# Measured durations in the planner of a two-layer hybrid decoder trunk

## The chip, the cores and the metric

The kernel runs on one core of a Trainium2 chip. The time is the device time of one execution in microseconds (us), and a version is judged by the median of its runs.

## What is computed

A decoder trunk of two layers on 512 tokens of width 1024, all in float32. The reference, cut to what matters:

```python
def hybrid_mixer(h, ...):
    proj = h @ w_in                       # 1024 -> q, k, v, z, xbc, dt
    q = partial_rotary(q); k = partial_rotary(k)
    attn = dilated_attention(q, k, v)     # 8 query heads on 2 kv heads
    xbc = jax.nn.silu(causal_depthwise_conv(xbc, conv_w, conv_b))
    dt = jax.nn.softplus(dt + dt_bias)
    y = ssd_chunked(xs, dt, -jnp.exp(a_log), bm, cm) + d_skip * xs
    y = rmsnorm(y * jax.nn.silu(z), ssm_norm)   # in two groups of 512
    return jnp.concatenate([attn, y], axis=-1) @ w_out

def reference(x, ...):
    h = x
    for layer in range(2):
        h = h + hybrid_mixer(rmsnorm(h, norm_mix), ...)
        t = rmsnorm(h, norm_ffn)
        h = h + (jax.nn.silu(t @ w_gate) * (t @ w_up)) @ w_down   # hidden width 2816
    return rmsnorm(h, final_norm)
```

## The kernel before

Features lie on the partitions and the 512 tokens along the free axis. A weight piece of 128 columns and an operand are each split into a rounded part and a rest (`whi` and `wlo`, `xh` and `xl`), and a k-tile of a product takes three matmuls of 128x128 by 128x512: `xh,whi`, `xl,whi`, `xh,wlo`. ScalarE makes `whi`, VectorE makes `wlo`. `block` (line 506) writes one output tile `acc` in units of two k-tiles, six matmuls. Nearly all of TensorE's work is such units.

In a layer the input projection comes first, in pieces, and in between stand the small products of the state space part (`ssd`: tiles `ee`, `xdt`, `hold`), of the gate (`gate`) and of attention (`scores`, `values`). The gate multiplies `xbc` by `z` on GpSimd, squares the products on ScalarE (`sq`), adds the squares on GpSimd, sums them over the partitions by a small matmul (`tr<-ones,sq`), makes `var` on VectorE and `rcol` (a power) on GpSimd, and spreads `rcol` to a row by four transposes (`tr<-ident,rcol`). In attention each head's scores (`tr<-kh,qs2` and `tr<-kl,qs2`) go through a reduction on VectorE (`sa`, `mx`), an exponential with a sum on ScalarE (`sa`, `den`), a reciprocal and a scaling on VectorE. Four scaled heads are transposed (`tr<-ident,sa`), copied to SBUF by ScalarE (`pt`), multiplied with the values (`hold<-pt,vk`), and split into `ath` (ScalarE) and `atl` (VectorE). During attention, units of the output projection fill TensorE: parts r = 1 and 2 (eight output tiles each, of two units) need no attention result, part r = 0 needs `ath` and `atl` of all four token blocks.

The order of all this is not written by hand. Every operation is put in a list with an engine, an assumed duration, a priority number and the tiles that it reads and writes. `schedule` (line 217) plays the list on a simple model of the engines: whenever an engine is free in the model, it takes the ready operation of the lowest number, if the pools have room. The order of starts in the model is the order in which the instructions are emitted, and on the chip each engine runs its own list in that order, waiting at each instruction for what it needs. The priority of a projection unit is `clock[0]`, which goes on by an assumed duration per matmul; the other operations have numbers that are set relative to it (`at`). So an assumed duration never takes time on the chip: it only moves instructions in the engines' lists. The pools bound how far one engine can run ahead: three `acc` and three `tr` banks in PSUM, three `whi` and three `wlo` tiles.

The durations stand in `dcost` (line 375; VectorE and GpSimd), `act` (line 408; ScalarE), `block` and `finish` (matmuls of 512 columns) and at the two powers on GpSimd (lines 554 and 1150).

Of the kernel before, what the change touches and what calls it, by code (L numbers as in the profile page):

```python
# [33 lines left out]
KTOK = 4  # L34
# [15 lines left out]
# columns of the constant array  # L50
# [3 lines left out]
# columns of the transposed parameter rows  # L54
# [32 lines left out]
# The program is written as a list of operations on virtual tiles. A list schedule over a simple  # L87
# model of the engines fixes the order in which they are emitted; every engine then runs its
# instructions in that order.
# [69 lines left out]
class VTile:  # L159
    """A tile that gets its place when its first operation is emitted."""  # L160
# [22 lines left out]
class Plan:  # L183
# [33 lines left out]
    def schedule(self, reserve, near):  # L217
        """Start times by a list schedule: per engine the ready operation of the lowest priority
        number, with the slots of the pools and the loads of activation tables in the model."""
# [3 lines left out]
        engines = {}  # L223
# [5 lines left out]
        first = {}  # L229
# [37 lines left out]
        order = []  # L267
# [55 lines left out]
def hybrid_trunk(  # L323
# [50 lines left out]
    # ---- operations  # L374
    def dcost(eng, o, ins, fast=False, ptrs=0):
        n = o.free
        if eng == "pool":
            return 2.25e-3 * n + 0.07
        psum = any(isinstance(v, View) and v.tile.psum for v in [o] + ins)
        return (0.52e-3 if fast and not psum else 1.04e-3) * n + 0.065 + 0.06 * (ptrs > 0)  # L380
# [27 lines left out]
    def act(o, a, func, scale=None, bias=None, accum=None):  # L408
# [15 lines left out]
        cost = 0.83e-3 * o.free + (0.053 if a.tile.psum else 0.093) + 0.093 * len(ptr)  # L424
        plan.add("act", cost, outs, [a] + ptr, fn, table=TABLE.get(func))

    def mms(outs, prods, each, prio=None):
        """prods: (out, lhsT, rhs, start, stop), or (out, in, identity) for a transpose."""
# [40 lines left out]
    # A chunk is one load; its pieces, 128 columns each, are split into float32r parts hi + lo.  # L469
# [36 lines left out]
    def block(segs, lead=LEAD, t=None, total=None, done=0):  # L506
        """One output tile: segs of (weight piece, operands, first and last k-tile)."""
        t = acc() if t is None else t
        total = total or sum(k1 - k0 for _, _, k0, k1 in segs)
        for pid, xl, k0, k1 in segs:  # L510
# [5 lines left out]
            for ka in range(k0, k1, 2):  # L516
# [8 lines left out]
                mms([t], pr, 0.2165, clock[0])  # L525
                clock[0] += len(pr) * 0.2165
# [4 lines left out]
    hT = [C([P, S], f"hT{k}") for k in range(KD)]  # L531

    class Norm:
        """Sum of squares over feature tiles, then 1/rms per token, as a row on all partitions."""
# [12 lines left out]
        def col(self):  # L547
# [6 lines left out]
            plan.add("pool", 0.96, [self.r], [v, nhalf],  # L554
# [19 lines left out]
    # the first operands, out of the token-major input  # L574
# [56 lines left out]
    # coefficient -exp(a_log) on the rows of the heads, zero on the others  # L631
# [10 lines left out]
    # d_skip spread over the 64 features of a head: column l * 8 + j for feature tile j  # L642
# [16 lines left out]
    # selectors in float32r: row of a head to its 64 features, and the fixed halves of the  # L659
    # operands of the decay products  # L660
# [77 lines left out]
    def layer(l, xs, norm):  # L738
# [13 lines left out]
        # x, B, C through the convolution  # L752
# [15 lines left out]
        if l == 0:  # L768
            # the second half of the input arrives while its first half is in use
# [6 lines left out]
        # dt: the 16 columns sit on the first 16 rows of each quadrant, their low parts on the others  # L776
        M = {}

        def dt_chain():
# [35 lines left out]
            # token-major dt and dt * exp(last - cumulative)  # L815
# [11 lines left out]
            # decay over a whole chunk, on all partitions  # L827
# [26 lines left out]
        # ---- state space part of a group of heads  # L854
# [60 lines left out]
        def gate(g, ta):  # L915
            """Gate and grouped norm; leaves y / rms in place of x."""
# [26 lines left out]
        # ---- attention operands  # L943
# [248 lines left out]
```

## Time and profile before

| what | us |
|---|---|
| runs before: median of 3 (lowest, highest) | 1343.31 (1338.26, 1344.51) |
| span of the profiled execution, first to last instruction | 1336.7 |
| mean granted TensorE clock, as a share of full speed | 0.995 |
| TensorE busy | 1310.3 |
| VectorE busy | 789.0 |
| ScalarE busy | 608.4 |
| GpSimd busy | 143.2 |

For the profiled execution the page gives the span and no longer time. The lowest run lies 1.6 us above that span, the median 6.6 us. A busy TensorE isn't one at its peak, since the ends of matmuls are modelled: a projection matmul is shown with 0.39 us, while the next one starts 0.23 us later. Layer 0's mixer (projection, state space part, attention) runs to about 300 us in the trace, its SwiGLU to about 680, layer 1's mixer to about 955, its SwiGLU and the final norm to the end. Names in the trace leave out the numbers of the tiles.

### The profile page before, as it was taken

The page shows a single profiled execution, that of the slowest core. Times are in us where ns is not written, and L with a number is a line of the kernel's source. Part 1 is how long each engine was busy: PE and PEld are TensorE (multiplying, and loading weights), DVE is VectorE, ACT ScalarE, POOL GpSimd, SP SyncE. Part 2 cuts the span into 40 slices and gives each one's busy share as a digit, 9 for nine tenths or more (in the row PEclk, how much of TensorE's full clock was granted, in tenths as well). Part 3 has the DMA queues.
Part 4 walks back from the last instruction along what each step waited for, and adds up shares of the span by engine and source line. Part 5 has one row for each costly group of instructions (what it writes and reads, how often), then busy time and mean ns, then how long its engine had stood idle before and what let it go on. Part 6 is the DMA issues. An engine that isn't in the chain of part 4 may idle for free.

```text
span 1336.7 us, 15604 instructions
## 1 busy us (share of the span) xinstructions
PE 1310.3 (98%) x6118; PEld 1053.4 (79%) x6118; DVE 789.0 (59%) x1312; ACT 608.4 (46%) x956; POOL 143.2 (11%) x111
## 2 busy tenths in 40 slices
PE   7999998999999999999999999999999999999997
PEld 6778777678888888888888777767788888888876
DVE  5996689766444334444469687887744433344443
ACT  5878755654332223223347686466532222232233
POOL 1002456000000000000000235520000000000000
PEclk9999999999999999999999999999999999999999
DMA  5221111222222232222322221111332323332141
GB/s 176 95 95 64 63 63 32 64 63 95 95 95 75 96 129 95 95 87 96 117 84 76 67 92 64 38 58 38 91 115 84 97 74 102 111 123 67 61 160 63
DMA packets 111744, 115.46 MB, mean 86 GB/s; under 512 B 4492, under 2 KB 102072, under 8 KB 111672
## 3 DMA queue, kind: packets, MB, share of 16 engines
q1 hardware_dynamic: 111672, 114.47, 26.7%
q8 instruction: 48, 0.79, 0.3%
q14 instruction: 24, 0.20, 0.0%
HBM read 112.37 MB, written 2.10 MB: 86 GB/s over the span
## 4 chain that ended last, share of the span: by engine, by line
PE 89%; DVE 5%; ACT 2%; POOL 2%; issue 1%; DMA 1%; SPq 0%; POOLq 0%; DVEq 0%; ACTq 0%
PE acc L436 79%; PE tr L436 4%; PE tr L434 3%; PE hold L436 3%; DVE qs L384 1%; DVE xbc L395 1%; DVE wlo L384 1%; ACT whi L421 1%; POOL qr L384 0%; DMA raw<-in_w_down_dram 0%; POOL xbc L384 0%; DMA x<-in_x_dram 0%; DVE qs L949 0%; DVE sa L390 0%; DVE sa L1007 0%
## 5 line engine op out<-in xcount | busy, mean ns | idle before, releaser
L436 PE MATMUL acc<-xh,whi 128*128 128x512 f32 x1584 | 628.2, 397 | 1.4 <-ACT whi L421 1.1
L436 PE MATMUL acc<-xl,whi 128*128 128x512 f32 x1584 | 618.6, 391 | 0.0
L436 PE MATMUL acc<-xh,wlo 128*128 128x512 f32 x1568 | 613.2, 391 | 0.3 <-DVE wlo L384 0.3
L421 ACT CAST whi<-raw 128x1024 fp32r<-128x1024 f32 (+4 forms) x260 | 224.0, 867 | 490.3 <-PE acc L436 455.9
L436 PEld LDWEIGHTS acc<-xh,whi 128*128 128x128 f32 x1584 | 298.3, 188 | 66.8 <-issue 5.5
L436 PEld LDWEIGHTS acc<-xh,wlo 128*128 128x128 f32 x1568 | 295.0, 188 | 64.2 <-DVE wlo L384 1.5
L436 PEld LDWEIGHTS acc<-xl,whi 128*128 128x128 f32 x1584 | 298.5, 188 | 59.2 <-issue 0.5
L384 DVE TENSOR_TENSOR wlo<-raw,whi 128x1024 fp32r<-128x1024 f32 (+4 forms) x251 | 258.7, 1035 | 63.0 <-ACT whi L421 62.3
L384 DVE TENSOR_TENSOR ga<-acc,rstd 128x512 f32<-128x512 f32 x44 | 30.4, 692 | 182.4 <-PE acc L436 181.8
L384 DVE TENSOR_TENSOR hT<-hT,acc 128x512 f32<-128x512 f32 x80 | 54.8, 685 | 109.0 <-PE acc L436 108.3
L423 ACT ACT_TABLE_LOAD x54 | 69.3, 1283 | 6.4 <-DVE pmix L401 3.5
L555 POOL TENSOR_TENSOR rcol<-var,nhalf 128x4 f32<-128x4 f32 x8 | 8.7, 1091 | 558.3 <-DVE var L390 558.3
L395 DVE SCALAR_TENSOR_TENSOR xbc<-cu,cvp,xbc 128x511 f32<-128x511 f32 (+2 forms) x72 | 58.5, 816 | 3.2 <-ACT xbc L423 2.3
L384 DVE TENSOR_TENSOR up<-acc,rstd 128x512 f32<-128x512 f32 x44 | 30.3, 688 | 45.0 <-PE acc L436 44.9
L421 ACT CAST xh<-ga 128x512 fp32r<-128x512 f32 x44 | 27.4, 623 | 58.4 <-DVE ga L384 58.4
L423 ACT ACTIVATE sa<-sa,mx 128x512 f32<-128x512 f32 (+3 forms) x64 | 36.0, 562 | 36.6 <-DVE mx L1007 35.1
L1151 POOL TENSOR_TENSOR fr<-fvar,nhalf 128x1 f32<-128x1 f32 x4 | 2.2, 547 | 356.9 <-DVE fvar L390 356.9
L384 DVE TENSOR_TENSOR xl<-ga,xh 128x512 fp32r<-128x512 f32 x44 | 30.3, 688 | 15.1 <-ACT xh L421 15.1
L1007 DVE CUSTOM_DVE_ANT_0 sa<-tr,cst 128x512 f32<-128x512 f32 (+3 forms) x64 | 30.5, 477 | 10.3 <-PE tr L436 10.1
L384 DVE TENSOR_TENSOR ga<-ga,up 128x512 f32<-128x512 f32 x44 | 30.3, 689 | 3.7 <-ACT ga L423 1.4
L384 DVE TENSOR_TENSOR ee<-ee,cbm 128x512 f32<-128x512 f32 x32 | 26.0, 817 | 6.9 <-ACT ee L423 6.9
L384 POOL TENSOR_TENSOR xbc<-xbc,er 128x384 f32<-128x384 f32 x16 | 20.1, 1258 | 83.3 <-DVE er L384 43.1
(203 smaller groups left out, 1184.9 us busy)
## 6 DMA issues: line engine op xcount, KB each, us to landing
raw<-in_w_in_dram SPq DMA_DIRECT2D x25, 1024.0 KB, 5.0
raw<-in_w_gate_dram SPq DMA_DIRECT2D x20, 1024.0 KB, 5.2
raw<-in_w_up_dram SPq DMA_DIRECT2D x20, 1024.0 KB, 5.3
raw<-in_w_down_dram SPq DMA_DIRECT2D x16, 768.0 KB, 4.3
raw<-in_w_out_dram SPq DMA_DIRECT2D x8, 1024.0 KB, 4.9
raw<-in_w_down_dram SPq DMA_DIRECT2D x12, 640.0 KB, 4.4
raw<-in_w_out_dram SPq DMA_DIRECT2D x8, 512.0 KB, 5.0
x<-in_x_dram SPq DMA_DIRECT2D x8, 256.0 KB, 4.6
```

Source lines behind the costliest of these rows:

```text
L384: lambda: ENG[eng].tensor_tensor(R(o), R(a), R(b), alu))
L395: lambda: nc.vector.scalar_tensor_tensor(R(o), R(a), R(s), R(b), op0, op1))
L421: nc.scalar.copy(R(o), R(a))
L423: nc.scalar.activation(R(o), R(a), func, **kw)
L434: nc.tensor.transpose(R(p[0]), R(p[1]), R(p[2]))
L436: nc.tensor.matmul(R(p[0]), R(p[1]), R(p[2]), start=p[3], stop=p[4])
L555: lambda: nc.gpsimd.tensor_tensor(R(self.r), R(v), R(nhalf), ALU.pow))
L1007: nc.vector.tensor_tensor_reduce(R(sa[:, 0:nk]), R(t[:, 0:nk]), R(cst[:, C_MASK + S - nk:C_MASK + S]), 1.0, 3e38, ALU.add, ALU.min, R(m))
L1151: lambda r=r, v=v: nc.gpsimd.tensor_tensor(R(r), R(v), R(nhalf[:, 0:1]), ALU.pow))
```

## The change

Only the durations that the plan assumes are other numbers. A matmul of 512 columns goes from 0.2165 to 0.2267 us, both as a duration and as the step of `clock[0]`. A VectorE operation gets a fixed part of 0.155 us in place of 0.065, and its fast form (one input, SBUF to SBUF) isn't assumed any more where a per-partition scalar is read. A ScalarE operation gets 0.10 us more. The two powers on GpSimd go from 0.96 to 1.09 and from 0.30 to 0.55 us. GpSimd's other operations, the scores' matmuls and the reductions keep theirs. The list of operations is the same. The diff (lines in which only a comment was taken out are not shown):

```diff
     def dcost(eng, o, ins, fast=False, ptrs=0):
...
-        return (0.52e-3 if fast and not psum else 1.04e-3) * n + 0.065 + 0.06 * (ptrs > 0)
+        return (0.52e-3 if fast and not psum and not ptrs else 1.042e-3) * n + 0.155 + 0.04 * (ptrs > 0)
...
-        cost = 0.83e-3 * o.free + (0.053 if a.tile.psum else 0.093) + 0.093 * len(ptr)
+        cost = 0.84e-3 * o.free + (0.155 if a.tile.psum else 0.19) + 0.1 * len(ptr)
...
-                mms([t], pr, 0.2165, clock[0])
-                clock[0] += len(pr) * 0.2165
+                mms([t], pr, 0.2267, clock[0])
+                clock[0] += len(pr) * 0.2267
...
-            plan.add("pool", 0.96, [self.r], [v, nhalf],
+            plan.add("pool", 1.09, [self.r], [v, nhalf],
...
-            plan.add("pool", 0.3, [r], [v, nhalf],
+            plan.add("pool", 0.55, [r], [v, nhalf],
```

What it does to the order is seen in the engines' lists. The list of weight loads keeps its order. In both SwiGLU parts and in the final product TensorE's list is the same, up to the first units after attention; all that moves lies in the two mixers, and the second layer moves much as the first. Three places follow, all in layer 0. In the names of these lists the first number tells tiles of one kind apart and is the same in both kernels; a second number counts tiles in the order of emission.

The first is ScalarE at the first gate's squares (`sq_291`, `sq_292`; `whi_237` is a coming weight piece, `xbc_223` a convolution that waits for VectorE). Before:

```order
L421 CAST whi_233_1266<-raw_203_1120 128x1024
L423 ACTIVATE xbc_223_1279<-cu_222_1269,cvp_61_361 128x512
L423 ACTIVATE sq_291_1284<-xbc_178_743 128x512
L423 ACTIVATE ee_352_1286<-tr_351_1271 128x512
L423 ACT_TABLE_LOAD
L423 ACTIVATE ee_352_1286<-ee_352_1286 128x512
L423 ACT_TABLE_LOAD
L423 ACTIVATE xbc_223_1279<-xbc_223_1279,cvp_61_361 128x512
L421 CAST whi_237_1325<-raw_203_1120 128x1024
L423 ACTIVATE sq_292_1327<-xbc_183_849 128x512
```

And the same engine and place in the changed kernel:

```order
L421 CAST whi_233_1272<-raw_203_1105 128x1024
L423 ACTIVATE xbc_223_1277<-cu_222_1274,cvp_61_359 128x512
L423 ACTIVATE ee_352_1290<-tr_351_1281 128x512
L423 ACT_TABLE_LOAD
L423 ACTIVATE ee_352_1290<-ee_352_1290 128x512
L423 ACTIVATE sq_291_1307<-xbc_178_773 128x512
L423 ACTIVATE sq_292_1316<-xbc_183_821 128x512
L421 CAST whi_237_1320<-raw_203_1105 128x1024
L423 ACTIVATE ee_359_1330<-tr_358_1305 128x512
```

The last square now stands before the convolution `xbc_223` and before the weight cast, where it stood behind both.

The second place is TensorE at the sum of the second gate's squares (`tr_397`), where attention's scores begin (`tr_420`, `tr_422`). Before:

```order
L436 MATMUL tr_397_1956<-ones_7_74,sq_393_1587 128x1 x4
L436 MATMUL tr_420_1969<-kh_306_1657,qs2_335_1915 128x512
L436 MATMUL tr_420_1969<-kl_307_1678,qs2_335_1915 128x512
L436 MATMUL acc_542_1940<-xh_530_1443,whi_543_1895 128x512
L436 MATMUL acc_542_1940<-xl_531_1457,whi_543_1895 128x512
L436 MATMUL acc_542_1940<-xh_530_1443,wlo_544_1898 128x512
L436 MATMUL acc_542_1940<-xh_532_1484,whi_543_1895 128x512
L436 MATMUL acc_542_1940<-xl_533_1491,whi_543_1895 128x512
L436 MATMUL acc_542_1940<-xh_532_1484,wlo_544_1898 128x512
L436 MATMUL tr_422_1986<-kh_306_1657,qs2_336_1919 128x512
L436 MATMUL tr_422_1986<-kl_307_1678,qs2_336_1919 128x512
L434 MATMUL tr_400_1994<-ident_1_72,rcol_399_1982 128x128 x4
```

And now, from the same sum on:

```order
L436 MATMUL tr_397_1952<-ones_7_74,sq_393_1593 128x1 x4
L436 MATMUL acc_542_1939<-xh_530_1440,whi_543_1895 128x512
L436 MATMUL acc_542_1939<-xl_531_1456,whi_543_1895 128x512
L436 MATMUL acc_542_1939<-xh_530_1440,wlo_544_1906 128x512
L436 MATMUL acc_542_1939<-xh_532_1458,whi_543_1895 128x512
L436 MATMUL acc_542_1939<-xl_533_1488,whi_543_1895 128x512
L436 MATMUL acc_542_1939<-xh_532_1458,wlo_544_1906 128x512
L436 MATMUL tr_420_1976<-kh_306_1645,qs2_335_1915 128x512
L436 MATMUL tr_420_1976<-kl_307_1666,qs2_335_1915 128x512
L436 MATMUL acc_545_1983<-xh_526_1416,whi_546_1903 128x512
```

The unit of `acc_542` stands ahead of the scores `tr_420`; behind the row of `acc_545` come five more of that unit, then `tr_400`, and `tr_422` follows it. So twelve projection matmuls lie between the sum and `tr_400`, where six did. From here on, units of the output projection are taken earlier throughout attention: by the first `hold<-pt,vk` eleven of them, where it was seven.

The third place is TensorE at the end of attention: the scores of the last head (`tr_519`), the last transposes (`tr_524`), the last product with the values (`hold_521`), and the first unit that needs all of attention (`acc_596`). Before, behind `tr_519`:

```order
L436 MATMUL tr_519_2617<-kh_306_1657,qs2_343_1966 128x128
L436 MATMUL tr_519_2617<-kl_307_1678,qs2_343_1966 128x128
L436 MATMUL acc_585_2599<-xh_564_2060,whi_586_2471 128x512
L436 MATMUL acc_585_2599<-xl_565_2081,whi_586_2471 128x512
L436 MATMUL acc_585_2599<-xh_564_2060,wlo_587_2488 128x512
L436 MATMUL acc_585_2599<-xh_566_2076,whi_586_2471 128x512
L436 MATMUL acc_585_2599<-xl_567_2133,whi_586_2471 128x512
L436 MATMUL acc_585_2599<-xh_566_2076,wlo_587_2488 128x512
L436 MATMUL acc_588_2633<-xh_560_2026,whi_589_2516 128x512
```

Six matmuls of `acc_588` then stand before `tr_524`, six between it and `hold_521`, and six of `acc_591` between `hold_521` and `acc_596`. In the changed kernel there are none of these:

```order
L436 MATMUL acc_591_2592<-xh_566_2086,wlo_593_2513 128x512
L436 MATMUL tr_519_2654<-kh_306_1645,qs2_343_1964 128x128
L436 MATMUL tr_519_2654<-kl_307_1666,qs2_343_1964 128x128
L434 MATMUL tr_524_2675<-ident_1_72,sa_514_2619 128x128
L434 MATMUL tr_524_2675<-ident_1_72,sa_516_2636 128x128
L434 MATMUL tr_524_2675<-ident_1_72,sa_518_2664 128x128
L434 MATMUL tr_524_2675<-ident_1_72,sa_520_2669 128x128
L436 MATMUL hold_521_2682<-pt_523_2650,vk_313_1670 64x512
L436 MATMUL hold_521_2682<-pt_525_2680,vk_313_1670 64x512
L436 MATMUL acc_596_2692<-ath_402_2277,whi_597_2526 128x512
```

`acc_591`, the last tile that needs no attention, ends just before `tr_519`, and nothing stands between the last links of the chain. On VectorE the list behind `acc_591` reads, in the changed kernel:

```order
L384 TENSOR_TENSOR hT7_18_234<-hT7_18_234,acc_591_2592 128x512
L384 TENSOR_TENSOR wlo_610_2661<-raw_594_2274,whi_609_2657 128x512
L1011 RECIPROCAL den_503_2548<-den_503_2548 128x1
L1007 ISA sa_518_2664,mx_504_2542<-tr_517_2626,cst_60_322 128x128
L1007 ISA mx_504_2542 128x1
L390 TENSOR_SCALAR sa_516_2636<-sa_516_2636,den_503_2548 128x128
L1011 RECIPROCAL den_503_2548<-den_503_2548 128x1
L1007 ISA sa_520_2669,mx_504_2542<-tr_519_2654,cst_60_322 128x128
L1007 ISA mx_504_2542 128x1
L390 TENSOR_SCALAR sa_518_2664<-sa_518_2664,den_503_2548 128x128
L1011 RECIPROCAL den_503_2548<-den_503_2548 128x1
L390 TENSOR_SCALAR sa_520_2669<-sa_520_2669,den_503_2548 128x128
```

These are the steps that make the four scaled heads which `tr_524` transposes, and an addition into the residual (`hT7`) and a weight split (`wlo_610`) stand at their head. Before, the same steps stood behind `hT4` and `wlo_593`, two output tiles earlier.

## Rows read from the trace of the kernel before

**Rows 1.** The page: span, and busy time of each engine.
```profile
span 1336.7 us, 15604 instructions
PE 1310.3 (98%) x6118; PEld 1053.4 (79%) x6118; DVE 789.0 (59%) x1312; ACT 608.4 (46%) x956; POOL 143.2 (11%) x111
```

**Rows 2.** Chain of waits over the whole span: start, duration, what.
```profile
322.44 354.99 PE acc L436 x1566
```

**Rows 3.** What TensorE waited for: total us, times, longest.
```profile
PE tr L436 <- POOL sq L384: 3.8, 4, 1.0
PE tr L436 <- ACT rstd L421: 1.4, 2, 0.7
```

**Rows 4.** Stretches: length, busy per engine (count), granted clock, DMA share, GB/s.
```profile
145.00:149.00 4.00, 4.00 (x21) 2.95 (x20) 2.64 (x5) 3.12 (x5) 2.08 (x2) 0.57 0.40 139
...
220.00:224.00 4.00, 3.18 (x9) 1.92 (x8) 3.90 (x11) 2.53 (x5) 1.32 (x1) 0.57 0.00 0
224.00:236.00 12.00, 11.32 (x57) 9.34 (x58) 11.91 (x27) 9.24 (x19) 5.71 (x4) 1.00 0.00 1
...
270.00:290.00 20.00, 20.00 (x100) 14.40 (x100) 12.13 (x50) 10.11 (x32) 0.00 (x0) 1.00 0.23 53
...
800.00:804.00 4.00, 4.00 (x28) 2.65 (x24) 2.46 (x4) 2.42 (x4) 2.53 (x3) 1.00 0.18 62
```

**Rows 5.** Timeline at the first gate, layer 0: start, duration, instruction, [idle before].
```profile
132.10 1.30 POOL L384 TENSOR_TENSOR xbc<-xbc,z 128x512 f32<-128x512 f32 x1
...
137.02 1.74 POOL L384 TENSOR_TENSOR xbc<-xbc,z 128x512 f32<-128x512 f32 x1
141.61 1.77 POOL L384 TENSOR_TENSOR sq<-sq,sq 128x512 f32<-128x512 f32 x1 [2.85 <-ACT sq L423]
...
139.34 0.72 ACT L423 ACTIVATE xbc<-xbc,cvp 128x512 f32<-128x512 f32 x1 [1.54 <-DVE xbc L395]
...
140.90 0.63 ACT L423 ACTIVATE sq<-xbc 128x512 f32<-128x512 f32 x1
...
142.04 0.40 PE L436 MATMUL acc<-xh,wlo 128*128 128x512 f32 x1
143.44 1.05 PE L436 MATMUL tr<-ones,sq 128*128 128x1 f32 x8 [1.00 <-POOL sq L384]
```

**Rows 6.** Timeline at the second gate, layer 0.
```profile
216.92 1.05 PE L436 MATMUL tr<-ones,sq 128*128 128x1 f32 x8 [0.93 <-POOL sq L384]
...
219.29 0.47 PE L436 MATMUL tr<-kh,qs 128*128 128x512 f32 x1 [1.32 <-DVE mx L1007]
...
222.37 0.15 DVE L390 TENSOR_SCALAR var<-tr 128x4 f32<-128x4 f32 x1
...
222.60 1.32 POOL L555 TENSOR_TENSOR rcol<-var,nhalf 128x4 f32<-128x4 f32 x1 [2.94 <-DVE var L390]
...
223.97 0.65 PE L434 MATMUL tr<-ident,rcol 128*128 128x128 f32 x4 [0.82 <-POOL rcol L555]
```

**Rows 7.** Timeline at the end of attention, layer 0.
```profile
279.32 0.68 DVE L384 TENSOR_TENSOR hT<-hT,acc 128x512 f32<-128x512 f32 x1
...
282.56 0.29 DVE L390 TENSOR_SCALAR sa<-sa,den 128x128 f32<-128x128 f32 x1
...
283.78 0.60 PE L434 MATMUL tr<-ident,sa 128*128 128x128 f32 x4
...
284.41 0.59 ACT L421 COPY pt<-tr 128x512 f32<-128x512 f32 x1 [1.37 <-PE tr L434]
...
285.71 1.08 PE L436 MATMUL hold<-pt,vk 128*64 128x512 f32 x4
...
286.86 0.43 ACT L421 CAST ath<-hold 128x128 fp32r<-128x128 f32 x2 [0.61 <-PE hold L436]
...
288.12 0.69 DVE L384 TENSOR_TENSOR atl<-hold,ath 128x128 fp32r<-128x128 f32 x3 [0.50 <-ACT ath L421]
...
291.00 0.62 ACT L421 CAST whi<-raw 128x512 fp32r<-128x512 f32 x1 [2.91 <-PE acc L436]
```

More of the change, by code (lines that the diff above doesn't have):

```diff
@@ L1138, in finish @@
                 for u in range(0, len(pr), 6):
-                    mms([t], pr[u:u + 6], 0.2165, clock[0])
-                    clock[0] += 6 * 0.2165
+                    mms([t], pr[u:u + 6], 0.2267, clock[0])
+                    clock[0] += 6 * 0.2267
                 at(clock[0])
```

## The prediction

> **What bounds the kernel now.** I read the page first: TensorE is busy in 1310.3 of 1336.7 us [rows 1], so only what stops TensorE can move the end. The chain of waits says the same: one piece of it is 1566 projection matmuls in 354.99 us [rows 2], 0.2267 us each with nothing between. Such stretches hold both SwiGLU parts, and there the order does not change. What can be won or lost lies in the two mixers, in TensorE's stops. The list of what TensorE waited for names the first: the sum of the gate's squares, four times, 3.8 us [rows 3], one at each gate of each layer. The stretches show what comes with a stop: behind the one at 142 us, and behind those at 216 to 219 us, the granted clock is 0.57 over 4 us [rows 4]. That is 3.4 us at the half level (1.2 GHz), and it costs up to 1.7 us where matmuls would run densely; I count 1.5. In layer 1 the first gate's stop has no such fall behind it (granted 1.00 at 800 to 804 us, [rows 4]). The timelines then give the details of three places, in which the order changes most.
>
> **Removed: the stop at the first gate.** TensorE's last projection matmul before it starts at 142.04, the next could start 0.23 later, and the sum starts at 143.44 [rows 5]: a stop of 1.2 us. It waited for GpSimd's last addition (141.61 to 143.38), this for ScalarE's square at 140.90, and this stood behind a convolution step at 139.34 and a weight cast, though its input, GpSimd's product, was done at 137.02 + 1.74 = 138.76 [rows 5]. In the new list the square stands ahead of both. GpSimd's six operations can then follow each other without the 2.85 us pause, and end 2.85 earlier, at 140.5. They start about one unit (6 x 0.2267 = 1.36 us) later, because the hold that feeds them stands one unit later in TensorE's list: 141.9. TensorE reaches the sum one unit later too, less the transposes that were moved behind it, at about 141.7. So some 0.2 us of the stop is left, a gain of 1.0, and in layer 0 the clock stays up, 1.5 more. Bounds: nothing gained (the stop is as long as before) and 1.2 + 1.7. I take 2.5 us in layer 0 and, with no fall to save, 1.0 in layer 1.
>
> **Moved: the second gate.** The sum starts at 216.92 in both orders: GpSimd, VectorE and ScalarE have the same order there, and TensorE waits for them. Behind it, `rcol` ends at 222.60 + 1.32 = 223.92, since `var` is at 222.37 behind the same VectorE instructions [rows 6]. TensorE had two pairs of scores and one unit to do until then; now it has one pair and two units. That is 1.36 more and 0.5 less, 0.9 gained. The stop of 0.7 behind `rcol`, for the row `rstd` [rows 3], is filled by the other pair and the next unit, 0.7 more: 1.6 us per layer. Bounds: 0 and 3.2 (the stops of 1.32, 0.82, 0.7 and some of the clock).
>
> **Moved: filler that VectorE must feed.** By the first product with the values the new order has used four more units. Each needs its `wlo` from VectorE (0.68 to 0.69 us, as in [rows 7] for a 512-wide operation with two inputs), and VectorE is busy 11.91 of 12 us there [rows 4]. So 4 x 0.68 = 2.7 us of its work now stands ahead of the scores' reductions, and TensorE's `tr` banks come free later. Some of it is met by slack, because the same reductions were early before; bounds 0 and 2.7, and I take 0.75 per layer, nearer to nothing since TensorE did not wait for these reductions after 226 us.
>
> **Added: the end of attention.** Before, TensorE is busy 20 of 20 us here [rows 4], because 24 projection matmuls stand between the last links. Now there are none, and the chain shows. VectorE starts with the addition of `hT7`, just when the last unit ends; then come `wlo_610`, two reductions, three reciprocals and three scalings. ScalarE must first cast `whi_609`, which waits for the last unit, since it takes the tile that this unit reads: the same cast is seen waiting for TensorE at 291.00 [rows 7]. The same VectorE sequence, with `hT4` and `wlo_593` at its head, ran in 279.32 to 282.85, 3.53 us [rows 7]. TensorE has 0.17 us of scores to do beside it. That leaves a stop of 3.5 us (0.15 of latencies on both sides). Then the transposes: their copy starts 0.63 after them and takes 0.59, so the second half of `hold` starts 1.22 after the transposes and not 0.9: 0.3. Then `ath` begins 1.15 behind the start of `hold`, and the second `atl` is done about 1.55 behind that (288.12 + 0.29 - 286.86) [rows 7], and it is needed by the fifth matmul of the first unit, which would have been issued 1.0 + 4 x 0.23 = 1.9 behind the start of `hold`, not 2.7: 0.9. Together 4.7 us per layer, hidden before by the filler and by nothing now. Bounds: 1.3 + 1.2 = 2.5, if only the last head's reduction, exponential and scaling (1.3 of the 3.5) come late; and 6. A stop three times as long as the one at 142 should also bring the clock down: 1.5 more per layer, bounds 0 and 3.
>
> **The sum.** Layer 0: -2.5 - 1.6 + 0.75 + 4.7 + 1.5 = +2.85. Layer 1: -1.0 - 1.6 + 0.75 + 4.7 + 1.5 = +4.35. Together +7.2 us, a span of 1343.9 for 1336.7. The runs lie 1.6 to 7.8 above that span; the median 6.6 above. Against the median of 1343.3 this is 1350.5, slower by 0.5%. The three fewer loads of activation tables (1.28 us each, on ScalarE) and the moves in the first 130 us are set at nothing: VectorE has room behind dense TensorE work there, and without that cover they would be worth about a us either way. The last product's and the final norm's lists do not move.
>
> **Rivals.**
> First, not slower: the reductions of the last heads are done early. If TensorE's stops up to there let VectorE get ahead, only the last head is late at the end of attention: 2.5 in place of 4.7, and with a short stop no fall of the clock: 3.7 less per layer, -0.2 in all, 1343. For it: VectorE has 8 us of slack in 20 there [rows 4]. Against it: the additions `hT7` and `wlo_610` stand ahead of the reductions in its list, and cannot start before the last unit ends. It decides where the stop before the last transposes is under 1.5 us.
> Second, faster: besides this, the second gate gives its full 3.2 and VectorE's lag is nothing: -0.2 - 2 x 1.6 - 2 x 0.75 = -4.9, and with 1.0 more at the gates of the state space part -7: 1336.
> Third, slower still: the stop at the first gate stays. GpSimd's product of one shape took 1.30 us at 132.10 and 1.74 at 137.02 [rows 5], beside a VectorE that was busier; the change leaves GpSimd's assumed durations and this spread as they are. If the now unbroken run of six meets VectorE's convolutions and ends 1.2 later than I count, the gain of 3.5 is gone: +10.7, 1354. The Trainium skill ("SBUF — State Buffer", section "Who interferes with whom") has a rule by which this would come about: a VectorE operation with two inputs in SBUF and a GpSimd operation that reads SBUF block each other for the whole instruction, so one duration for each can't be right. The two durations of one shape agree with that rule.
> Fourth, slower still: VectorE's lag costs its 2.7 and the clock stays low longer behind the last stop (3 in place of 1.5): +7.2 + 2 x 1.95 + 2 x 1.5 = +14, 1357.
>
> **How the numbers follow.** Forecast, +3 to +11 around 1350.5: 0.50. First rival 0.20, second 0.12, third 0.10, fourth 0.08. About 0.5% (6.7 us) is what a measurement of this kernel can tell from no change. Of the forecast's 0.50, 0.30 lies above that and 0.20 below it; the third and fourth are slower; the first is the same but for 0.05 faster; of the second 0.08 is faster. That makes slower 0.48, the same 0.39, faster 0.13. Range 1338 to 1358; the forecast's own 1346 to 1354.
>
> **What would show it.** In the changed profile: a TensorE wait of 3 us or more for the scaling (`sa`, line 390) before the last transposes, in each layer, near 285 and 940 us, and a granted clock near 0.6 behind it; no wait for the gate's `sq` at 142 and granted 1.00 behind it; the wait for `mx` at 219 gone, that for `rcol` still there. The forecast is wrong if the stop at the end of attention is under 1.5 us, or if TensorE stops elsewhere for more than 5 us in all that it did not before.

## The result and the profile after

The changed kernel takes 1348.22 us (median of 9 runs, 1347.07 to 1350.85), the kernel before 1341.52 us (9 runs, 1337.33 to 1344.69). The ratio is 1.0058, with a 95% interval of 1.0040 to 1.0075: slower by 0.6%, where 1350.5 was forecast. The runs of the kernel before lie in two groups, near 1338 and near 1343.5, and its profiled execution is one of the lower; spans are therefore compared below with spans, and medians by the ratio to runs of the kernel before on the same chip.

The page of the changed kernel:

```profile
span 1345.3 us, 15613 instructions
PE 1310.8 (97%) x6118; PEld 1052.2 (78%) x6118; DVE 797.6 (59%) x1312; ACT 602.9 (45%) x953; POOL 145.7 (11%) x111
```

Against [rows 1], TensorE is busy as long as before (1310.8 us for 1310.3), and the span is 8.6 us longer: nearly all of it is time in which TensorE stood still. What it waited for, over the whole span (total us, times, longest; a cut):

```profile
PE hold L436 <- DVE ee L384: 6.3, 7, 2.3
PE tr L434 <- DVE sa L390: 4.8, 6, 1.3
PE tr L434 <- POOL rcol L555: 4.0, 3, 1.6
...
PE tr L436 <- POOL sq L384: 1.8, 2, 0.9
```

Two of the four waits for the gate's squares of [rows 3] are gone (3.8 us then, 1.8 now), and the waits for `rstd` and `mx` too. New are the waits for `sa`, three in each layer, and the longer ones for `ee` and `rcol`.

To see where each microsecond goes, I add up what TensorE loses: the time from the start of one matmul to the next, less the usual step of that kind of matmul (the lower quartile of its steps in these two traces). In dense stretches it is nearly nothing; around short matmuls some is left in every kernel, so only differences count. A matmul slowed by a lower clock counts as a loss too. In us, both layers added where nothing else is said:

| stretch | before | after | difference | forecast |
|---|---|---|---|---|
| start to first gate, layer 0 | 18.45 | 20.99 | +2.5 | 0 |
| first gates (layer 0, layer 1) | 4.27 + 2.89 | 1.63 + 2.49 | -2.6, -0.4 | -2.5, -1.0 |
| state space part between the gates | 13.89 | 17.66 | +3.8 | 0 |
| second gates | 14.72 | 11.38 | -3.3 | -3.2 |
| attention, to the last scores | 23.82 | 23.60 | -0.2 | +1.5 |
| end of attention (layer 0, layer 1) | 1.36 + 1.37 | 6.86 + 5.97 | +5.5, +4.6 | +6.2, +6.2 |
| the rest | 10.71 | 9.58 | -1.1 | 0 |
| sum | 91.5 | 100.2 | +8.7 | +7.2 |

The forecast for the ends of attention holds its 1.5 us of clock. The end of attention in the changed kernel, layer 0 (start, duration, instruction, [idle before]):

```profile
287.92 0.28 DVE L390 TENSOR_SCALAR sa<-sa,den 128x128 f32<-128x128 f32 x1
...
287.98 0.27 PE L436 MATMUL tr<-kl,qs 128*128 128x128 f32 x1
288.12 0.69 DVE L384 TENSOR_TENSOR hT<-hT,acc 128x512 f32<-128x512 f32 x1
288.34 0.30 PE L434 MATMUL tr<-ident,sa 128*128 128x128 f32 x1
...
288.73 0.68 DVE L384 TENSOR_TENSOR wlo<-raw,whi 128x512 fp32r<-128x512 f32 x1
...
289.33 0.16 DVE L1011 RECIPROCAL den<-den 128x1 f32<-128x1 f32 x1
289.40 0.27 DVE L1007 CUSTOM_DVE_ANT_0 sa<-tr,cst 128x128 f32<-128x128 f32 x1
...
289.60 0.28 DVE L390 TENSOR_SCALAR sa<-sa,den 128x128 f32<-128x128 f32 x1
...
289.94 0.33 PE L434 MATMUL tr<-ident,sa 128*128 128x128 f32 x1 [1.29 <-DVE sa L390]
...
290.86 0.33 PE L434 MATMUL tr<-ident,sa 128*128 128x128 f32 x1 [0.59 <-DVE sa L390]
...
291.70 0.33 PE L434 MATMUL tr<-ident,sa 128*128 128x128 f32 x1 [0.52 <-DVE sa L390]
291.96 2.71 PE L436 MATMUL hold<-pt,vk 128*64 128x512 f32 x4
...
295.03 0.69 PE L436 MATMUL acc<-ath,whi 128*128 128x512 f32 x1 [0.35 <-ACT ath L421]
```

In [rows 7] the same chain ran beside projection matmuls and cost nothing. Now the addition into `hT7` and the split `wlo` stand ahead of the reductions, as the order said, and each of the last three transposes waits by itself for its scaled head. And the windows (length, busy per engine (count), granted clock, DMA share, GB/s):

```profile
145.00:149.00 4.00, 4.00 (x25) 2.83 (x25) 4.00 (x7) 3.94 (x5) 1.03 (x1) 1.00 0.49 146
...
220.00:224.00 4.00, 4.00 (x12) 3.00 (x12) 3.97 (x10) 2.67 (x6) 1.39 (x1) 0.57 0.13 51
...
292.00:296.00 4.00, 3.65 (x8) 1.21 (x8) 0.49 (x2) 1.28 (x4) 0.00 (x0) 0.57 0.00 0
...
950.00:954.00 4.00, 3.65 (x14) 2.07 (x12) 1.07 (x4) 0.96 (x4) 0.00 (x0) 1.00 0.00 0
```

Against [rows 4], the granted clock is 1.00 behind the first gate, 0.57 still behind the second, and 0.57 behind the end of attention in layer 0. There it was 1.00 before:

```profile
286.00:292.00 6.00, 6.00 (x27) 4.36 (x24) 2.91 (x8) 1.74 (x6) 0.00 (x0) 1.00 0.12 24
```

In layer 1 the same chain leaves it at 1.00. The two ends lose the same up to the last transpose; the 0.9 us between them comes from there on, where in layer 0 the clock is low.

### The profile page after: what moved, and what is told of

Read it like the earlier page. It is cut to its first block, busy times and chain, and to the rows that moved or that the text cites. A ratio compares the mean times of both kernels' runs of the same rounds, so it can differ in the third digit from the quotient of the medians.

```text
span 1345.3 us, 15613 instructions
## 1 busy us (share of the span) xinstructions
PE 1310.8 (97%) x6118; PEld 1052.2 (78%) x6118; DVE 797.6 (59%) x1312; ACT 602.9 (45%) x953; POOL 145.7 (11%) x111
## 4 chain that ended last, share of the span: by engine, by line
PE 86%; DVE 9%; ACT 2%; POOL 1%; issue 1%; DMA 1%; SPq 0%; POOLq 0%; ACTq 0%; DVEq 0%
PE acc L436 77%; PE tr L436 3%; PE hold L436 3%; PE tr L434 3%; DVE wlo L384 2%; DVE xbc L395 1%; DVE qs L384 1%; DVE ee L384 1%; DVE qr L384 1%; ACT whi L421 1%; POOL xbc L384 0%; POOL qr L384 0%; DVE qs L949 0%; DMA x<-in_x_dram 0%; ACT sa L423 0%
## 5 line engine op out<-in xcount | busy, mean ns | idle before, releaser
L384 DVE TENSOR_TENSOR wlo<-raw,whi 128x1024 fp32r<-128x1024 f32 (+4 forms) x251 | 261.6, 1048 | 60.5 <-ACT whi L421 59.6
L395 DVE SCALAR_TENSOR_TENSOR xbc<-cu,cvp,xbc 128x511 f32<-128x511 f32 (+2 forms) x72 | 62.0, 864 | 2.9 <-ACT xbc L423 2.4
L434 PEld LDWEIGHTS tr<-ident,sa 128*128 128x128 f32 x160 | 18.8, 140 | 13.4 <-DVE sa L390 7.6
```

The lines of the kernel that those rows point to most:

```text
L384: lambda: ENG[eng].tensor_tensor(R(o), R(a), R(b), alu))
L395: lambda: nc.vector.scalar_tensor_tensor(R(o), R(a), R(s), R(b), op0, op1))
L434: nc.tensor.transpose(R(p[0]), R(p[1]), R(p[2]))
```

## The experiments

Theory A: the ends are empty because the plan keeps VectorE for longer. The operations' durations as the trace shows them are not the time for which the engine is taken. In the rows above a scaling of 0.28 us is followed by the next operation 0.20 later, one of 0.69 by the next 0.61 later (288.12, 288.73), a reciprocal of 0.16 by the next 0.07 later. With the old fixed part of 0.065 us the plan assumes 0.60 us for 512 columns of two inputs, which is that step; with the new one, 0.155, it assumes 0.69, which is the shown duration. Theory B: every longer number has its share.

**One part at a time.** Each is the kernel before with one part of the diff that stands above. The two powers on GpSimd, a fourth part, were not run alone.

```diff
-                mms([t], pr, 0.2165, clock[0])
-                clock[0] += len(pr) * 0.2165
+                mms([t], pr, 0.2267, clock[0])
+                clock[0] += len(pr) * 0.2267
...
```

> Only the matmuls' 0.2267 us, every other assumed duration as before. Theory A (VectorE's longer assumed occupation spends the filler early, nothing else does): five units stand behind the last scores, so TensorE stops there under 0.5 us in either layer, and what the run loses or wins against before lies in the state space part and at the gates; 1337 to 1347. Theory B (every stretch of the plan has its share of the 10 us lost at the two ends of attention): a stop of 1 to 2 us at either end and about 1345.

```diff
-        return (0.52e-3 if fast and not psum else 1.04e-3) * n + 0.065 + 0.06 * (ptrs > 0)
+        return (0.52e-3 if fast and not psum and not ptrs else 1.042e-3) * n + 0.155 + 0.04 * (ptrs > 0)
```

> Only VectorE's assumed durations as changed, the rest as before. Theory A: no unit stands behind the last scores in either layer, TensorE stops there for 3 us or more, and the ends of attention lose 9 to 11 us against before, as in the changed kernel; 1346 to 1353. Theory B: a third of that, 1344 or 1345.

```diff
-        cost = 0.83e-3 * o.free + (0.053 if a.tile.psum else 0.093) + 0.093 * len(ptr)
+        cost = 0.84e-3 * o.free + (0.155 if a.tile.psum else 0.19) + 0.1 * len(ptr)
```

> Only ScalarE's assumed durations as changed, the rest as before. Theory A: the ends of attention keep their units (one between the last transposes and the last product, four ahead of them) and TensorE stops there under 1.5 us; 1338 to 1346. Theory B: a third of the loss at either end, 3 us in all, 1344 or 1345.

**Latency apart.** The changed kernel, but the added fixed parts delay only the reader.

```diff
-        return (0.52e-3 if fast and not psum and not ptrs else 1.042e-3) * n + 0.155 + 0.04 * (ptrs > 0)
+        return (0.52e-3 if fast and not psum and not ptrs else 1.042e-3) * n + 0.065 + 0.04 * (ptrs > 0)
...
-                 lambda: ENG[eng].tensor_tensor(R(o), R(a), R(b), alu))
+                 lambda: ENG[eng].tensor_tensor(R(o), R(a), R(b), alu), lat=0.09 * (eng == "dve"))
...
-        cost = 0.84e-3 * o.free + (0.155 if a.tile.psum else 0.19) + 0.1 * len(ptr)
-        plan.add("act", cost, outs, [a] + ptr, fn, table=TABLE.get(func))
+        cost = 0.84e-3 * o.free + (0.055 if a.tile.psum else 0.09) + 0.1 * len(ptr)
+        plan.add("act", cost, outs, [a] + ptr, fn, table=TABLE.get(func), lat=0.1)
```

> As the changed kernel, but the 0.09 us added to each VectorE operation and the 0.10 us added to each ScalarE operation are a latency: the plan lets the reader wait for them and takes the engine as free. Theory A (the plan's mistake is that it keeps the engine for the whole duration): four units stand ahead of the last transposes again, no stop over 1.5 us at either end of attention, and 8 to 12 us less than the changed kernel: 1336 to 1341. Rival C (the longer chain from reduction to transposes, latency and all, is what spends the filler): stops of 3 us and more remain at the ends, 1346 to 1350.

Losses of TensorE as above, in us (the first gates are left out); the ratio is to the kernel before on the same chip, where its median was 1337.96, with its 95% interval:

| | median | ratio | to first gate | between gates | second gates | attention | ends | rest |
|---|---|---|---|---|---|---|---|---|
| matmuls only | 1350.75 | 1.0091 (1.0074, 1.0107) | 21.8 | 16.0 | 17.7 | 24.8 | 3.1 | 11.4 |
| VectorE only | 1357.50 | 1.0144 (1.0127, 1.0162) | 26.3 | 15.0 | 12.6 | 25.9 | 12.7 | 13.3 |
| ScalarE only | 1349.51 | 1.0083 (1.0068, 1.0099) | 20.8 | 18.7 | 15.2 | 23.5 | 4.1 | 15.9 |
| latency apart | 1338.69 | 0.9998 (0.9986, 1.0009) | 19.9 | 17.2 | 10.7 | 23.9 | 4.4 | 10.6 |

On the ends theory A is right: VectorE's numbers alone empty them (12.7 us, as 12.8 in the changed kernel), the other two leave them near the 2.7 of before, and with the latencies apart they lose 4.4. That run's total was also as theory A said. On the totals of the three parts the forecasts of both theories missed: the matmuls' number alone and ScalarE's alone cost 8 to 9 us in other places, and VectorE's alone cost more than either theory allowed. With the matmuls' number the second gate of layer 0 gets two long stops:

```profile
PE tr L434 <- POOL rcol L555: 3.4, 1, 3.4
PE tr L436 <- POOL sq L384: 2.3, 1, 2.3
```

(what TensorE waited for from 200 to 300 us). With ScalarE's, the state space part between the gates rises from 13.9 to 18.7, more than the changed kernel's 17.7, and the rest rises by 5 us, 4.0 of them waits in the last product and the final norm. The parts are no sum: together they cost no more than the cheapest of the three alone (spans of 1345.3 us for 1345.9, 1347.0 and 1355.8).

**Units given back to the end.** The changed kernel; four units may not be planned ahead of the last head's scores (a dependency in the plan alone, `A["last"]` being the last scores' operation).

```diff
+        o = plan.add("pe", each * len(prods), outs, ins, fn, prio, lat=0.08)
+        if after is not None:
+            o.deps.add(after)
+            after.users.append(o)
...
-                t = block([(po[k], xo, 0, 4)])
+                t = block([(po[k], xo, 0, 4)], after=A["last"] if r == 2 and k >= 6 else None)
```

> The changed kernel, in which the plan may not place the last two output tiles of part r = 2 (four units) before the last head's scores; the plan is the same up to those. Theory A (the ends cost what they do because no unit is left for them): the four units cover the chain again, under 1.5 us of stop before the last transposes, the two ends lose 2 us each in place of 6.9 and 6.0, and the run takes 1339 to 1341. Rival D (VectorE's chain bounds all of attention): TensorE stops earlier, where the units are missing now, for 1.5 us or more in each layer, and the gain is 3 us or less: 1345 to 1348.

It took 1350.83 us, 1.0069 (1.0046, 1.0091): theory A is wrong about the cure. Rival D is right that TensorE stops earlier instead, though the run gained nothing and lies above D's 1345 to 1348 too. The ends fell to 5.7, attention rose from 23.6 to 34.8. What TensorE waited for from 276 to 290 us, where the changed kernel had no stop of note before the last scores:

```profile
PE tr L436 <- ACT pt L421: 1.9, 2, 1.6
PE tr L434 <- DVE mx L1011: 0.8, 1, 0.8
PE tr L434 <- ACT pt L421: 0.7, 1, 0.7
```

From the third token block's first scores to the last scores of all, TensorE took 25.8 us in the changed kernel with 54 projection matmuls, 26.0 us here with 30, and 27.2 us in the kernel before with 60. With 30 or with 54 matmuls it is about 26 us: I read this as the chain's own pace.

**VectorE's numbers in attention alone.** The old or new numbers are used only from attention's first scores to the end of the output projection; first in the kernel before:

```diff
+        if slow[0]:
+            return (0.52e-3 if fast and not psum and not ptrs else 1.042e-3) * n + 0.155 + 0.04 * (ptrs > 0)
         return (0.52e-3 if fast and not psum else 1.04e-3) * n + 0.065 + 0.06 * (ptrs > 0)
...
+        slow[0] = True
         ta = tq
...
+        slow[0] = False
         at(clock[0])
```

> The kernel before with VectorE's changed durations for the operations from attention's first scores to the end of the output projection alone (scalings, atl, additions into the residual, splits of operands and of weights), the state space part and the gates keeping the old ones. Theory A: empty ends in both layers, 4.5 to 5.5 us each, less 1.5 us each at the second gate, where the list behind the gate's sum is nearly the changed kernel's: 6 to 8 us above the kernel before, 1344 to 1346. Rival: without the state space part's share the ends are filled in time, and it stays within 3 us of the kernel before.

and, the other way about, the old ones in the changed kernel:

```diff
+        if slow[0]:
+            return (0.52e-3 if fast and not psum else 1.04e-3) * n + 0.065 + 0.06 * (ptrs > 0)
         return (0.52e-3 if fast and not psum and not ptrs else 1.042e-3) * n + 0.155 + 0.04 * (ptrs > 0)
...
```

> The changed kernel with VectorE's old durations for those operations alone. Theory A: three units stand ahead of the last transposes, no stop over 1.5 us at either end, and 8 to 10 us less than the changed kernel: 1338 to 1341. Rival: ScalarE's and the matmuls' new numbers empty the ends by themselves, or the stops move into attention; 1344 or more.

The first took 1351.9 us, 1.0075 (1.0052, 1.0098), more than theory A said, and its ends lose 13.2 us: attention's numbers are enough to empty them. The second took 1346.26, 1.0036 (1.0020, 1.0051), where A said 1338 to 1341. Its ends lose 5.4, but the second gates 14.9 in place of 11.4 and attention 25.5 in place of 23.6: a stop of 2.2 us for `mx` and one of 2.0 for `qs` in its list of waits. Of the 7.4 us saved at the ends most is lost again in these places.

**Where units are free.** Theory E: a unit is paid in full where TensorE is dense anyway, in the first half of attention, and is free where the chain sets the pace. The first run keeps part r = 2 out of the first half, in the changed kernel (the dependency as above):

```diff
-                t = block([(po[k], xo, 0, 4)])
+                t = block([(po[k], xo, 0, 4)], after=A[1, 0] if r == 2 else None)
```

> The changed kernel, in which the plan may not place part r = 2 (sixteen units) before the third token block's first scores. From the second gate's sum to those scores stand 66 projection matmuls, where the changed kernel has 108 and the kernel before 72; behind the last scores stand 30 again. Theory E (a unit taken in the first half of attention, where TensorE has no gap, is paid in full; one taken later is free up to the chain's own pace of 26 us from the third block to the last scores and 7 us behind them): the first half shrinks from 42.7 to 34 to 37 us, the ends lose 2 us, gate to first unit with attention's result takes 70 to 72 us in place of 75, and the run takes 1338 to 1342. Rival F (VectorE's list, with its additions and splits ahead of the reductions, sets the pace): stops of 3 us and more per layer open in the first half, where the units were, and it stays at 1347 to 1351.

The other two are the kernel before, with the units' number lowered and no duration touched:

```diff
-                mms([t], pr, 0.2165, clock[0])
+                mms([t], pr, 0.2165, clock[0] - early)
...
-                t = block([(po[k], xo, 0, 4)])
+                t = block([(po[k], xo, 0, 4)], early=4.0 if r else 0.0)
```

> The kernel before with nothing changed but the number by which the units of parts r = 1 and 2 are picked: 4 us earlier. By the third block's first scores 96 projection matmuls are placed and not 72, and 12 are left behind the last scores and not 24 and 6 more. Theory E: some 18 to 24 more matmuls are paid for at 0.2267 us, 4 to 5.4 us per layer less up to 1.6 at the second gate: 5 to 9 us above the kernel before in all. Rival F (nothing but VectorE's assumed durations spoils the order): within 3 us of the kernel before.

> The same with 8 us: 18 matmuls already ahead of the second gate's sum, 84 from there to the third block, none behind the last scores. Theory E: all 30 of the end are paid for earlier, 6.8 us per layer, less up to 3 at the second gate: 8 to 13 us above the kernel before, with stops of 3 us and more before the last transposes. Rival F: within 3 us of it.

In layer 0, in us from the second gate's sum on (its second group; the count is of projection matmuls that far):

| | third block's scores | last scores | first unit with attention's result | span | median, ratio |
|---|---|---|---|---|---|
| before | 36.3 us, 72 | 63.5, 132 | 70.8, 156 | 1336.7 | |
| changed | 42.7, 108 | 68.5, 162 | 75.5, 162 | 1345.3 | 1348.22, 1.0058 |
| kept from first half | 36.5, 66 | 64.8, 126 | 73.5, 156 | 1343.0 | 1345.86, 1.0033 (1.0019, 1.0047) |
| 4 us earlier | 43.2, 96 | 69.1, 150 | 74.8, 162 | 1342.1 | 1342.33, 1.0011 (0.9998, 1.0024) |
| 8 us earlier | 42.2, 84 (and 18 ahead of the sum) | 69.3, 144 | 76.2, 144 | 1349.5 | 1351.16, 1.0072 (1.0051, 1.0093) |

In the two last the ends lose 5.6 and 13.4 with no duration changed at all. The second of them took 9.2 us more than the kernel before, as E said and against F. The first can't be told from the kernel before by its time (1341.97 there), which was F's forecast; its span stands 5.4 above that of before, but with a granted clock of 0.992 for 0.995, so that a part of this is the clock. Whether 4 us earlier costs time stays open. The run kept from the first half is neither theory's. It took 1345.86, where E said 1338 to 1342 and F 1347 to 1351: the ends lose 2.7, as before the change, yet of the 6.5 us by which second gates, attention and ends together lose more than before only 2.2 come back. The first half takes 36.5 us with 66 matmuls, no less than 36.3 with 72, with stops of 1.15 us for `sa` and 0.68 for `pt` in it:

```profile
253.26 0.33 PE L434 MATMUL tr<-ident,sa 128*128 128x128 f32 x1 [1.15 <-DVE sa L390]
254.26 0.45 PE L436 MATMUL tr<-kh,qs 128*128 128x384 f32 x1 [0.68 <-ACT pt L421]
```

So the units' place alone can empty the ends and cost 9 us, but giving them back recovers only 2.2 of 6.5 us. That the rest lies in the lists that feed TensorE (VectorE's and ScalarE's), which the new numbers reordered as well, fits these two stops but is not shown; which rows of those lists it would be stays open.

**GpSimd in the plan.** The run with the latencies apart, and longer GpSimd operations: 512 columns are assumed at 1.45 us in place of 1.22.

```diff
-            return 2.25e-3 * n + 0.07
+            return 2.7e-3 * n + 0.07
```

> The run with the latencies apart, and GpSimd's 512-wide operations assumed at 1.45 us in place of 1.22 (the traces show 1.26 to 1.77, the longer ones beside VectorE). If the stops left at the second gate (1.9 us for the sum of the squares, 0.8 and 1.9 for rcol) come from the plan's too short GpSimd, they shrink to 1 us or less in sum per layer and the run gains 3 to 6 us: 1333 to 1336, below both kernels. If they are the chain's own length, with no unit left to put there, it stays at 1337 to 1340.

> The run with the latencies apart, and GpSimd's 512-wide operations assumed at 1.32 us, between 1.22 (which left a stop of 1.9 us for the sum of the squares) and 1.45 (which put the small var operation 4.9 us behind the sum on VectorE and cost a stop of 3.3 us). If the second gate's loss has its least between the two, it falls under 5 us per layer and the run takes 1334 to 1336; if the order jumps with every number, it lands anywhere from 1336 to 1346.

The first took 1337.75 us, 0.9973 (0.9957, 0.9988): below both medians, but above the hoped 1333 to 1336, and no faster than the kernel before at the same granted clock (all twelve runs had 0.995 or 0.996; with 0.995 the kernel before took 1337.3 to 1339.0 on this chip). Between the gates it loses 13.9, as before the change and 3.3 less than with 1.22 us; the second gates got worse, 14.4 for 10.7, since the small `var` now stands 4.9 us behind the sum:

```profile
PE tr L436 <- DVE var L390: 6.3, 2, 3.1
```

The middle value (2.45e-3 for 2.7e-3, 1.32 us) took 1340.52, 0.9993 (0.9979, 1.0008), not the least of the three: the order jumps with the number. So a single run of a new order proves little. But all three with the latencies apart took 1337.8 to 1340.5, and the changed kernel and the seven other runs that use its numbers, whole or in part, 1345.9 to 1357.5.

## Why the prediction came out

**First gates, right in layer 0.** GpSimd's run of six operations is unbroken now, where [rows 5] showed 2.85 us of idle time:

```profile
134.86 2.00 POOL L384 TENSOR_TENSOR xbc<-xbc,er 128x384 f32<-128x384 f32 x2 [15.97 <-DVE xbc L395]
136.81 4.00 POOL L384 TENSOR_TENSOR xbc<-xbc,z 128x512 f32<-128x512 f32 x2
...
140.76 3.45 POOL L384 TENSOR_TENSOR sq<-sq,sq 128x512 f32<-128x512 f32 x2
...
144.36 0.95 PE L436 MATMUL tr<-ones,sq 128*128 128x1 f32 x8
```

The last addition ends at 144.21 and the sum follows. From first start to last end the six took 9.4 us, and the forecast had counted 9.5 (143.38 - 131.00 - 2.85, the first of them starting at 131.00 before), so they were not slower in sum, as the third rival had it, though the last four took 1.7 to 2.0 us each. But they began 3.9 us later than before and not 1.36, and ended 2.3 later than forecast. TensorE hardly waited because it reached the sum 2.7 later than forecast too (144.4 for 141.7). The clock stayed up, as forecast. In layer 1 the gain was 0.4 for 1.0: the stop at the sum went there too, but TensorE now stops 1.1 us for `rcol` behind it, which the prediction did not look for.

**Second gates, right.** In layer 0 it reads now:

```profile
219.02 1.05 PE L436 MATMUL tr<-ones,sq 128*128 128x1 f32 x8 [0.91 <-POOL sq L384]
...
226.25 0.65 PE L434 MATMUL tr<-ident,rcol 128*128 128x128 f32 x4 [1.26 <-POOL rcol L555]
```

Against [rows 6], the wait for `mx` between the two is gone, that for `rcol` is still there (1.26 for 0.82), and the net is -1.7 and -1.65 for -1.6 each.

**VectorE's lag, over-sized.** It was forecast at 0.75 per layer and measured -0.1: the lower bound was right. From the second gate to the last scores TensorE loses no more than before; its waits for `sa` all stand at the end, where the lag had been counted already.

**End of attention, right in place and kind, a little too large.** One stop of 3.5 us was forecast; three came, 1.48, 0.81 and 0.74 by the steps, 3.0 in all, for the last three scalings come one after another and the transposes follow each. The 0.9 behind the last product was 1.2 in layer 0, at the lower clock, and 0.7 in layer 1. The clock fell in one layer and not in both.

**The state space part, wrong.** That "the moves in the first 130 us are set at nothing" is the step that failed: it was +2.5 us up to the first gate, and +3.8 between the gates, of which the prediction did not speak at all. It named as its own limit "if TensorE stops elsewhere for more than 5 us in all that it did not before", and these 6.3 us pass it; the total was right by luck, because the ends (2.3), the lag (1.7) and the rest (1.1) came out lower by about as much. That the 2.5 us come from the order, and not from one execution to the next, is seen in the other runs: three whose lists are those of the kernel before until 197 us or later (attention's numbers alone, 4 and 8 us earlier) lose between 1.0 less and 0.9 more than it up to the first gate; three that share the changed kernel's lists there (units kept, kept from first half, attention's numbers back) lose 2.4 to 3.1 more.

There was luck in the time as well. The forecast put the median 6.6 us above the span, as it was in three runs of the kernel before. In the changed kernel it lies 2.9 above (1348.22 and 1345.3). So the span forecast, 1343.9, was 1.4 too low and the time, 1350.5, 2.3 too high.

The largest of these stops, in the changed kernel:

```profile
158.87 0.68 DVE L384 TENSOR_TENSOR z<-acc,rstd 128x512 f32<-128x512 f32 x1
159.47 0.67 DVE L384 TENSOR_TENSOR state<-state,tr 128x512 f32<-128x512 f32 x1
160.06 1.21 DVE L384 TENSOR_TENSOR wlo<-raw,whi 128x1024 fp32r<-128x1024 f32 x1
161.20 1.53 DVE L395 SCALAR_TENSOR_TENSOR xl<-xbc,prm,xh 128x512 fp32r<-128x512 f32 x1
162.65 0.68 DVE L384 TENSOR_TENSOR state<-state,tr 128x512 f32<-128x512 f32 x1
163.25 0.68 DVE L384 TENSOR_TENSOR ee<-ee,cbm 128x512 f32<-128x512 f32 x1
...
163.98 0.66 PE L436 MATMUL hold<-ee,xdt 128*64 128x128 f32 x8 [2.28 <-DVE ee L384]
```

and the same product's operand on VectorE in the kernel before:

```profile
157.55 0.67 DVE L384 TENSOR_TENSOR state<-state,tr 128x512 f32<-128x512 f32 x1
158.14 0.68 DVE L384 TENSOR_TENSOR ee<-ee,cbm 128x512 f32<-128x512 f32 x1
158.75 1.21 DVE L384 TENSOR_TENSOR wlo<-raw,whi 128x1024 fp32r<-128x1024 f32 x1
159.88 0.74 DVE L395 SCALAR_TENSOR_TENSOR xl<-xbc,prm,xh 128x512 fp32r<-128x512 f32 x1
```

There `ee` stood ahead of `wlo` and `xl`; now it stands behind both, and `xl` takes twice as long beside a GpSimd operation. The waits for `ee` between the gates grew by 2.3 us in layer 0 (1.1 and 3.4). That ScalarE's numbers are enough for this part is shown by the runs (18.7 us with those alone, 15.0 and 16.0 with the others); why the plan then puts `ee` later was not traced.

The prediction also never asked whether a shown duration is the time for which an engine is taken. The trace of [rows 7] would have told it: the addition of 0.68 us at 279.32 there overlaps its successor by 0.08.

```profile
279.92 0.69 DVE L384 TENSOR_TENSOR wlo<-raw,whi 128x512 fp32r<-128x512 f32 x1
```

The Trainium skill says the same ("Perfetto Trace Analysis", section "Optimizing Scalar/DVE Operations"): about 60 ns of an operation's fixed cost keep VectorE busy, and the profiled latency has about twice that, because the acknowledgement of the write overlaps with the next instruction. The steps above (0.20 for 0.28, 0.61 for 0.69) agree, and the run with the latencies apart shows what the difference is worth to this plan: 7.9 us of the spans (1345.3 and 1337.4), 9.5 of the medians (1348.22 and 1338.69, not timed side by side).

## What to carry to other kernels

In a planner's cost table an operation has two numbers, how long it keeps its engine and when its result is there; take the first from the distance between two starts in a busy run, and the second from the shown duration. Filler that is used in a stretch without gaps is paid for: here 36 more matmuls, 8.2 us by their step of 0.2267, took the first half of attention from 36.3 to 42.7 us. So ask of each new order which stretch loses its cover and which gains work it has no gap for. A place that got better in such a change says little about the sum: give each stretch its own row, also those that the argument does not speak of.

## What the runs showed of the hardware

The changed plan assumes no fast form for a VectorE operation that reads a per-partition scalar: 0.73 us for a scaling of 512 columns. By shape, such scalings in the changed kernel (count | busy us, mean ns):

```profile
L390 DVE TENSOR_SCALAR sa<-sa,den 128x512 f32<-128x512 f32 x16 | 11.6, 723 | 0.1
L390 DVE TENSOR_SCALAR sa<-sa,den 128x384 f32<-128x384 f32 x16 | 6.7, 417 | 0.1
```

The mean of the first fits that number, but it mixes two things: beside GpSimd's products (227.60 to 233.46) one takes 1.52 us, and after them one takes 0.47:

```profile
227.60 5.86 POOL L384 TENSOR_TENSOR xbc<-xbc,rstd 128x512 f32<-128x512 f32 x4 [1.41 <-ACT rstd L421]
...
230.80 1.52 DVE L390 TENSOR_SCALAR sa<-sa,den 128x512 f32<-128x512 f32 x1
...
235.86 0.47 DVE L390 TENSOR_SCALAR sa<-sa,den 128x512 f32<-128x512 f32 x1
```

Of the 16, twelve take 0.47 to 0.52 and four 1.35 to 1.52. The four lie wholly beside GpSimd operations; of the twelve, six lie beside one for a part of their time and six beside none. A mean of a group is no duration to plan with where two engines hinder each other.

The changed kernel's runs spread by 3.8 us with their granted clock: spans of 1345.3 us at a mean of 0.997, 1349.1 at 0.992. The kernel before does the same. Of its 69 executions timed beside the experiments, 35 had a mean granted clock of 0.994 to 0.996 and took 1337.0 to 1339.5 us; 34 had 0.989 to 0.993 and took 1341.5 to 1345.2. The twelve of the run with the latencies apart had 0.995 to 0.998 and took 1337.1 to 1339.2. Why one order keeps the clock up in every execution and another in half of them is not shown.
